# Output projection in token-major blocks with summed pairs, and a sixth summed pair and a residual in PSUM for down: a Hymba layer on one core

## The chip, the cores and the metric

One core of one Trainium2 chip runs the whole program. The metric is the device time of one execution in microseconds; several executions are taken, and the median of them is the kernel's time. The profile is of one further execution, and has a time of its own. The engines are TensorE (PE; PEld is its weight load), VectorE (DVE), ScalarE (ACT), GpSimd (POOL) and SyncE (SP), which here issues nearly all DMAs.

## The reference

One decoder layer, sequence 256, model width 2048, feed-forward width 5632, all in float32:

```python
u = rmsnorm(h)
[lru_x | lru_gate | q | k | v | ret_gate] = u @ W_in
A = rg_lru(causal_conv(lru_x)) * gelu(lru_gate)        # 1024 wide
B = group_norm(retention(q, k, v)) * swish(ret_gate)   # 1024 wide
h = h + concat(A, B) @ W_out                           # the output projection
n = rmsnorm(h)
h = h + (silu(n @ W_gate) * (n @ W_up)) @ W_down       # SwiGLU
out = rmsnorm(h)
```

## The kernel before

Every product of two float32 matrices is done in three passes. Both sides are split into a high part (a cast on ACT, L103, tiles `wh`, `ah`, `bh`) and the rest (a subtraction on DVE, L104, tiles `wl`, `al`, `bl`), and PE adds high x high, high x low and low x high into one PSUM bank (`three`, L653). The weights stream in halves of 512 KB, 128 x 1024 numbers, over SP's queue into five raw buffers (`raw`) and four pairs of split buffers. The program is a list of steps, each with the weight units that it needs; the loads and splits of a step are written out three halves ahead of it (`AHEAD`). A scheduler then sets the order of each engine's instructions by its own estimates, so that the order on an engine is not that of the code.

The steps are, with their time in the profile: the projections of `u` to v, lru_x, k, q, the gates, with scan and retention between them, to 293.4 us; the output projection to 383.8; eleven gate/up blocks to 858.3; two down blocks to 1088.5; the last norm and the stores.

The output projection is feature-major: 16 tiles of 128 features by 256 tokens (`fm_tile` with `w_out`). For each of the 16 slices of y a tile takes one matmul with 512 columns (the high and the low part of y side by side, L144) and one with 256 (L145); the last two tiles take three of 256 (L149 to L151). `out_post` adds the two halves of the bank, adds the result to the residual x in its feature-major tiles, scales a copy of it on ACT (`hf`), splits that into the left sides of the gate/up blocks (`Left`, `hh`), and adds up squares, which two matmuls against ones sum over the features (`norm2`, tile `rms`). Later `resid_tok` turns the residual to token-major with 32 transposes (tile `ht`), since the down blocks add to it in that form.

Gate/up and down blocks are token-major: a block has four PSUM banks `c11`, `c12`, `c21`, `c22` of 128 tokens x 512 columns (first digit: the half of the tokens; second: gate or up, or the left or right 512 columns), and runs over quads, 256 rows of weights by 1024 columns each. A plain quad is 8 products of 128 x 128 by 128 x 512 (`EIGHT`), thus 24 matmuls. A summed pair, as Strassen and Winograd did, has 7 products (21 matmuls) on sums of quarters; DVE makes the sums of the weights (L636, four adds) and of the left side (L536 to L539, tile `s`), which are split as well. From the second gate/up block on, the summed pairs of a block run in two parts: a shared part, four products into four banks that are then combined by four DVE adds (L764 to L768, tiles `p`, `q`), done among the steps of the block before, and a direct part of three products. Block and neighbour take turns with two sets of four banks (`room`). The first gate/up block has one summed pair, in another form, and the others have three or four. A down block has 22 quads, five of them summed (`SUMMED_DOWN`); their results go through `part` tiles and the residual tiles `htok`.

At the end of the second down block the last bank, `c22`, is done in two halves (`c22`, `c22b`). `post` adds them to the residual (L930, L932, L935), `down_post` squares the sum on ACT (L956), works out r = 1/sqrt and a correcting step (L968 to L973), and scales four tiles by r (L978 to L988) and by the last norm's weight `fw`, partly on GpSimd ahead of time (L958). The stores are L989.

Of the kernel before, what the change touches and what calls it, by code (L numbers as in the profile page):

```python
# [31 lines left out]
SUMMED = (2, 3, 4)  # L32
SUMMED_MORE = (1, 2, 3, 4)
SUMMED_FIRST = (2,)
SUMMED_DOWN = (2, 5, 8, 11, 14)
# [3 lines left out]
def tile_hymba_layer(ctx: ExitStack, tc: tile.TileContext, A: dict, out: bass.AP):  # L39
# [4 lines left out]
    apool = ctx.enter_context(tc.tile_pool(name="acts", bufs=58))  # L44
    xpool = ctx.enter_context(tc.tile_pool(name="resid", bufs=10))
# [15 lines left out]
    def act_tile(name, dt=F32):  # L61
        return apool.tile([P, 512], dt, tag="act", name=nm(name))

# [329 lines left out]
    y = [None] * KT  # L393

    def lru_out(n, ps):
# [109 lines left out]
    def ret_y(h):  # L505
        ps = aux("yt")
        for t in range(2):
            o = oo[2 * t + h // 4][:, (h % 4) * P : (h % 4) * P + P]
            pe.transpose(ps[:, t * P : t * P + P], o, ident)
        hl = act_tile("y", F32R)  # L510
        g = gnh[:, h : h + 1]
        act.activation(out=hl[:, :S], in_=ps[:, :S], func=AF.Copy, scale=g)
        v.scalar_tensor_tensor(
            out=hl[:, S:], in0=ps[:, :S], scalar=g, in1=hl[:, :S].bitcast(F32), op0=ALU.mult, op1=ALU.subtract
        )
        y[NLRU + h] = hl
# [3 lines left out]
    hf = [None]  # L520
# [28 lines left out]
    def out_post(f, ps):  # L549
        x = xs(f)  # L550
        if f < KT - 2:
            t = act_tile("op")[:, :S]
            halves(ps, t)
            v.tensor_tensor(out=x, in0=x, in1=t, op=ALU.add)
        else:
            v.tensor_tensor(out=x, in0=ps[:, :S], in1=x, op=ALU.add)
        if f % 2 == 0:
            hf[0] = act_tile("hf")
        act.activation(out=hf[0][:, (f % 2) * S : (f % 2) * S + S], in_=x, func=AF.Copy, scale=col(C_LN2 + f))
        if f % 2:  # L560
            hh[f // 2] = Left(hf[0], f // 2 in SUMMED_MORE)
        sq = sumsq[:, :S] if f == 0 else act_tile("sq")[:, :S]
        act.activation(out=sq, in_=x, func=AF.Square)
        if f:
            v.tensor_tensor(out=sumsq[:, :S], in0=sumsq[:, :S], in1=sq, op=ALU.add)

    def norm2():
        ps = room(1)("rms")
        for t in range(2):
            pe.matmul(ps[:, 2 * t : 2 * t + 2], sumsq[:, t * P : t * P + P], ones[:, 0:2], start=True, stop=True)  # L570
        rsqrt_small(r2_tok, ps[:, 0:4:2], 1.0 / D, 2)

    htok = {}

    def resid_tok(cb, room):
        for t in range(2):
            ps = room("ht")
            for i in range(4):
                pe.transpose(ps[:, i * P : i * P + P], xs(4 * cb + i)[:, t * P : t * P + P], ident)  # L579
            htok[(cb, t)] = xpool.tile([P, 512], F32, tag="xh", name=nm("htok"))  # L580
            act.copy(out=htok[(cb, t)], in_=ps)
# [78 lines left out]
    def block(index, quads, lefts, post, ps, tail=(), after=None, between={}, ordered=False):  # L660
# [7 lines left out]
        for c, c0, cw in tail:  # L668
            todo += [(n, c, a, b, c0, cw, i) for i in range(n, len(quads)) for o, a, b in EIGHT if o == c[:3]]
        firsts, lasts = {}, {}  # L670
        for m, (_, c, *_) in enumerate(todo):
            firsts.setdefault(c, m)
            lasts[c] = m
        at = [0]

        def step(i):
            def run():
                while at[0] < len(todo) and todo[at[0]][0] == i:
                    m, (_, c, a, b, c0, cw, *q) = at[0], todo[at[0]]
# [8 lines left out]
                if after:  # L688
                    after(i)
# [51 lines left out]
    def gu(j, i):  # L741
        return A["w_gu"][j * (KT // 2) + i]

    banks = [{} for _ in range(NB)]
    turns = []
    summed = [SUMMED_MORE if j in (2, 4, 6, 8) else SUMMED for j in range(NB)]
    shared = [[Shared(gu(j, i), True) for i in summed[j]] for j in range(NB)]

    def shared_steps(j):

        ps, n = banks[j], len(summed[j])

        def run(m):
            right = shared[j][m].parts
            for c, a, b in (("c11", "a11", "b11"), ("c22", "s1", "t1"), ("c21", "s3", "t3"), ("c12", "s2", "t2")):
                if m == 0:
                    ps[c] = room(j)(c)
                three(ps[c], hh[summed[j][m]][a], right[b], m == 0, m == n - 1)
            if m < n - 1:
# [10 lines left out]
        return [([shared[j][m]], lambda m=m: run(m)) for m in range(n)]  # L770

    def gate_up(j):

        ps, post = banks[j], ffn_post(j, banks[j])
        ahead = shared_steps(j + 1) if j + 1 < NB else []
        plain = [i for i in range(KT // 2) if i not in summed[j]]

        def direct(m, quad):
# [421 lines left out]
```

## Time and profile before

| | us |
|---|---|
| median of 3 runs (1098.54, 1097.71, 1098.88) | 1098.54 |
| the profiled execution: its time | 1099.06 |
| the profiled execution: its span | 1097.3 |
| PE busy, share of the span | 99% |
| weight load of PE | 83% |
| DVE | 84% |
| ACT | 59% |
| GpSimd | 5% |

The time of the profiled execution holds 1.76 us around its span. PE's busy share is a share of time in which some matmul was under way; matmuls overlap, so it does not tell how many more PE could do. Lines of code in the profile's rows are those of this kernel, and a tile's name stands without its number.

### The profile page before, as it was taken

To read this page: it belongs to the slowest core of one execution; us is meant where nothing else is said; L and a number is where in the kernel's file an instruction comes from. 1 tells how busy PE (TensorE), PEld (TensorE's weight loads), DVE (VectorE), ACT (ScalarE), POOL (GpSimd) and SP (SyncE) were. 2 spreads that over 40 slices of the span, in tenths; PEclk is the share of its full clock that TensorE was granted. 3 is DMA by queue.
4 is the path that set the end of the run, shared out by engine and by line. 5 is a ranking of instruction groups with operands and counts; after the bars stand their busy time and mean duration, and the time that the engine had idled before them with its cause. 6 is when DMAs were issued, how large, how long until landed. Compare 5 with 4: busy or idle time off the path is not lost.

```text
span 1097.3 us, 14827 instructions
## 1 busy us (share of the span) xinstructions
PE 1086.0 (99%) x5289; PEld 914.5 (83%) x5289; DVE 917.4 (84%) x1307; ACT 645.9 (59%) x918; POOL 57.4 (5%) x64
## 2 busy tenths in 40 slices
PE   9999999999999999999999999999999999999996
PEld 7888888888888988888888888888888888878885
DVE  7798799987877799998898998998885989777773
ACT  7766644478665566665565556556654666454552
POOL 0602230000000000000000000000000000020001
PEclk9999999999999999999999999999999999999999
DMA  9755574554565547677677677686686555746662
GB/s 329 239 193 162 171 256 162 171 183 163 177 228 191 185 156 275 209 234 260 218 242 254 218 264 240 228 280 225 229 268 216 174 182 191 241 143 210 222 212 76
DMA packets 67114, 232.56 MB, mean 212 GB/s; under 512 B 7648, under 2 KB 8032, under 8 KB 67040
## 3 DMA queue, kind: packets, MB, share of 16 engines
q1 hardware_dynamic: 66240, 229.52, 62.8%
q0 software_dynamic: 512, 1.57, 0.5%
q8 instruction: 41, 0.67, 0.2%
q10 hardware_dynamic: 288, 0.52, 0.1%
q14 instruction: 33, 0.27, 0.1%
HBM read 229.49 MB, written 2.10 MB: 211 GB/s over the span
## 4 chain that ended last, share of the span: by engine, by line
PE 98%; DVE 1%; DMA 0%; ACT 0%; issue 0%; SPq 0%; DVEq 0%; ACTq 0%
PE c L657 20%; PE c L658 20%; PE c L656 20%; PE fm L144 16%; PE fm L145 8%; PE tm L160 3%; PE tm L161 3%; PE tm L162 3%; PE p L658 1%; PE p L657 1%; PE p L656 1%; PE ft L847 1%; PE fm L151 0%; PE fm L150 0%; PE fm L149 0%; PE ht L579 0%
## 5 line engine op out<-in xcount | busy, mean ns | idle before, releaser
L103 ACT CAST wh<-raw 128x1024 fp32r<-128x1024 f32 (+1 forms) x475 | 451.1, 974 | 356.9 <-DVE raw L636 118.9
L104 DVE TENSOR_TENSOR wl<-raw,wh 128x1024 fp32r<-128x1024 f32 (+1 forms) x475 | 530.4, 1140 | 113.0 <-ACT wh L103 109.0
L657 PE MATMUL c<-wl,ah 128*128 128x512 f32 x770 | 299.3, 390 | 0.8 <-DVE wl L104 0.8
L658 PE MATMUL c<-wh,al 128*128 128x512 f32 x770 | 298.7, 389 | 0.0
L656 PE MATMUL c<-wh,ah 128*128 128x512 f32 x770 | 248.8, 391 | 0.2 <-ACT wh L103 0.2
L144 PE MATMUL fm<-u,wh 128*128 128x512 f32 x512 | 179.9, 396 | 0.0
L657 PEld LDWEIGHTS c<-wl,ah 128*128 128x128 f32 x770 | 144.5, 188 | 31.2 <-DVE wl L104 1.6
L656 PEld LDWEIGHTS c<-wh,ah 128*128 128x128 f32 x770 | 144.1, 188 | 30.9 <-ACT wh L103 1.6
L658 PEld LDWEIGHTS c<-wh,al 128*128 128x128 f32 x770 | 144.5, 188 | 30.0
L145 PE MATMUL fm<-u,wl 128*128 128x256 f32 x512 | 143.4, 280 | 0.0
L144 PEld LDWEIGHTS fm<-u,wh 128*128 128x128 f32 x512 | 96.0, 188 | 22.3
L145 PEld LDWEIGHTS fm<-u,wl 128*128 128x128 f32 x512 | 96.5, 189 | 0.2
L144 PE MATMUL fm<-y,wh 128*128 128x512 f32 x224 | 78.8, 397 | 0.0
L636 DVE TENSOR_TENSOR raw<-raw,raw 128x512 f32<-128x512 f32 x90 | 62.2, 691 | 3.3 <-DMA raw<-in_w_gu 0.9
L636 DVE TENSOR_TENSOR raw<-raw 128x512 f32<-128x512 f32 x90 | 62.1, 690 | 2.3
L145 PE MATMUL fm<-y,wl 128*128 128x256 f32 x224 | 62.5, 281 | 0.0
L657 PE MATMUL c<-wl,sh 128*128 128x512 f32 x147 | 57.2, 389 | 0.0
L658 PE MATMUL c<-wh,sl 128*128 128x512 f32 x147 | 57.2, 389 | 0.0
L958 POOL TENSOR_TENSOR htok<-htok,fw 128x512 f32<-128x512 f32 (+1 forms) x7 | 9.5, 1368 | 899.1 <-ACT junk L956 899.1
L144 PEld LDWEIGHTS fm<-y,wh 128*128 128x128 f32 x224 | 41.9, 188 | 10.1
L656 PE MATMUL c<-wh,sh 128*128 128x512 f32 x147 | 49.9, 392 | 0.0
L161 PE MATMUL tm<-wl,u 128*128 128x512 f32 x128 | 49.4, 398 | 0.0
(253 smaller groups left out, 1201.6 us busy)
## 6 DMA issues: line engine op xcount, KB each, us to landing
raw<-in_w_gu SPq DMA_DIRECT2D x210, 512.0 KB, 5.1
raw<-in_w_down SPq DMA_DIRECT2D x88, 512.0 KB, 4.5
raw<-in_w_out SPq DMA_DIRECT2D x32, 512.0 KB, 4.1
raw<-in_w_lx SPq DMA_DIRECT2D x16, 512.0 KB, 4.3
raw<-in_w_k SPq DMA_DIRECT2D x16, 512.0 KB, 3.9
raw<-in_w_q SPq DMA_DIRECT2D x16, 512.0 KB, 4.3
raw<-in_w_rg SPq DMA_DIRECT2D x16, 512.0 KB, 3.8
raw<-in_w_lg SPq DMA_DIRECT2D x16, 512.0 KB, 3.8
```

The source lines that it names most:

```text
L103: act.copy(out=dst_h, in_=src)
L104: v.tensor_tensor(out=dst_l, in0=src, in1=dst_h.bitcast(F32), op=ALU.subtract)
L144: pe.matmul(ps, wh, hl, start=first, stop=False)
L145: pe.matmul(ps[:, :S], wl, hl[:, :S], start=False, stop=last)
L160: pe.matmul(ps, ah, wh, start=first, stop=False)
L161: pe.matmul(ps, ah, wl, start=False, stop=False)
L162: pe.matmul(ps, al, wh, start=False, stop=last)
L636: v.tensor_tensor(out=dst, in0=a, in1=b, op=ALU.add)
L656: pe.matmul(p, ah, bh, start=first, stop=False, skip_group_check=onto)
L657: pe.matmul(p, ah, bl, start=False, stop=False, skip_group_check=onto)
L658: pe.matmul(p, al, bh, start=False, stop=last, skip_group_check=onto)
L847: pe.transpose(pt[:, o : o + P], g[:, (2 * b + c) * P : (2 * b + c) * P + P], ident)
```

## The change

The output projection becomes two blocks like those of gate/up, of 8 quads each: `w_out` is packed in quads, y is kept as eight pairs of 256 features, split by `Left`, and the second block has two summed pairs, (4, 5). The class `Block` serves all thirteen blocks; `STEPS` gives the order of plain (p), direct (d) and shared (s) steps, an s being a shared part of the next block. The first gate/up block is in the two-part form too, with two summed pairs instead of one. The others keep their number of three or four, with other pairs chosen.

The residual x is loaded a second time, token-major, into `htok` (eight DMAs, new input `x_tok`). `out_post` adds a PSUM bank to it and squares the sum on ACT with an accumulator; the matmuls of `norm2` and the sums of squares on DVE go. `turn` transposes the new residual to feature-major, scales it on ACT and makes the left sides; the transposes of `resid_tok` go.

The down blocks have six summed pairs. In the second one the residual of `c22` is added in PSUM by DVE while products are still to come (`early`), the other half by way of ACT and DVE into `c22b` (`half_over`), whose first product is done ahead of `c11`. `down_post` then reads PSUM directly; the product r x w moves to GpSimd (`rw`) with two-scalar forms on DVE, one multiply by `fw` moves from GpSimd to DVE, and one of the last scalings is shared by DVE and ACT.

The diff, cut to its core:

```diff
-SUMMED = (2, 3, 4)
-SUMMED_MORE = (1, 2, 3, 4)
-SUMMED_FIRST = (2,)
-SUMMED_DOWN = (2, 5, 8, 11, 14)
+SUMMED = ((), (4, 5), (2, 3)) + ((1, 2, 3), (0, 1, 2, 3)) * 4 + ((1, 2, 3), (1, 2, 3))
+SUMMED_OUT, SUMMED_FFN = (4, 5), (0, 1, 2, 3)
+PLAIN = ((4, 5, 6, 7, 0, 1, 2, 3),) * 2 + (tuple(range(8)),) * 11
+STEPS = ("pppspppspp", "pdppsdpspp", "pdpsdpspspp") + ...
+SUMMED_DOWN = (2, 5, 8, 11, 14, 17)
...
+        cb, t = divmod(n, 2)
+        htok[cb, t] = res_tile("htok")
+        nc.sync.dma_start(out=htok[cb, t], in_=A["x_tok"][t * P : t * P + P, cb * 512 : cb * 512 + 512])
...
+        def turn(p):
+            pt, f = room(d)("ht"), act_tile("hf")
+            for c in range(2):
+                for t in range(2):
+                    h = htok[p // 2, t][:, (p % 2) * S + c * P : (p % 2) * S + c * P + P]
+                    pe.transpose(pt[:, c * S + t * P : c * S + t * P + P], h, ident)
+            for c in range(2):
+                cs = slice(c * S, c * S + S)
+                act.activation(out=f[:, cs], in_=pt[:, cs], func=AF.Copy, scale=col(C_LN2 + 2 * p + c))
+            hh[p] = Left(f, p in SUMMED_FFN)
+        def post(c, ps):
+            cb, t = 2 * d + int(c[2]) - 1, int(c[1]) - 1
+            h = htok[cb, t]
+            v.tensor_tensor(out=h, in0=ps, in1=h, op=ALU.add)
+            act.activation(out=act_tile("junk"), in_=h, func=AF.Square, accum_out=sq2[:, t, cb : cb + 1])
+            if t:
+                turns.extend(lambda p=p: turn(p) for p in (2 * cb, 2 * cb + 1))
...
+        def half_over():
+            h = htok[3, 1][:, S:]
+            act.copy(out=h, in_=ps["c22"][:, S:])
+            v.tensor_tensor(out=ps["c22b"][:, S:], in0=ps["c22b"][:, S:], in1=h, op=ALU.add)
+        if d:
+            early["c22"] = lambda: v.tensor_tensor(out=ps["c22"], in0=ps["c22"], in1=htok[3, 1], op=ALU.add)
+            early["c22b"] = half_over
+            tail[:0] = [("c22b", S, S, slice(0, 1))]
+            tail += [("c22", 0, S), ("c22b", S, S, slice(1, 4))]
...
-        v.tensor_scalar(out=r, in0=w, scalar1=r, scalar2=None, op0=ALU.mult)
+        rw = rw3[:, t : t + 1]
+        pool.tensor_tensor(out=rw, in0=r, in1=w, op=ALU.mult)
...
-    for f in range(KT):
-        fm_tile(Unit(A["w_out"][f]), y, order, lambda ps, f=f: out_post(f, ps), one=f >= KT - 2)
+    blocks = [Block(d, lambda i, d=d: A["w_out"][8 * d + i], y, out_post(d), STEPS[d]) for d in range(2)]
```

Three places of the program, before and after. VectorE in the output projection, before: weight splits, and between them one summed left side.

```order
L104 TENSOR_TENSOR wl_705_3603<-raw_703_3601,wh_704_3602 128x1024
L104 TENSOR_TENSOR al_688_3532<-hf_677_3476,ah_687_3531 128x512
L536 TENSOR_TENSOR s_689_3535<-hf_677_3476 128x128
L538 TENSOR_TENSOR s_689_3535<-hf_677_3476 128x128
L537 TENSOR_TENSOR s_689_3535<-hf_677_3476,s_689_3535 128x128
L539 TENSOR_TENSOR s_689_3535<-hf_677_3476,s_689_3535 128x128
L104 TENSOR_TENSOR wl_708_3609<-raw_706_3607,wh_707_3608 128x1024
L104 TENSOR_TENSOR sl_691_3541<-s_689_3535,sh_690_3540 128x512
```

After, where the first block of the output projection ends and the second begins (L583 adds a bank to the residual, L109 is the split):

```order
L583 TENSOR_TENSOR htok_578_2908<-c12_654_3251,htok_578_2908 128x512
L583 TENSOR_TENSOR htok_595_2982<-c22_655_3255,htok_595_2982 128x512
L109 TENSOR_TENSOR wl_721_3581<-raw_719_3578,wh_720_3580 128x1024
L109 TENSOR_TENSOR wl_728_3623<-raw_726_3620,wh_727_3622 128x1024
L109 TENSOR_TENSOR wl_731_3629<-raw_729_3626,wh_730_3628 128x1024
L109 TENSOR_TENSOR al_735_3653<-hf_733_3645,ah_734_3652 128x512
L549 TENSOR_TENSOR s_736_3656<-hf_733_3645 128x128
L551 TENSOR_TENSOR s_736_3656<-hf_733_3645 128x128
L550 TENSOR_TENSOR s_736_3656<-hf_733_3645,s_736_3656 128x128
L552 TENSOR_TENSOR s_736_3656<-hf_733_3645,s_736_3656 128x128
L109 TENSOR_TENSOR wl_762_3743<-raw_760_3740,wh_761_3742 128x1024
L109 TENSOR_TENSOR sl_738_3662<-s_736_3656,sh_737_3661 128x512
```

The left sides of the gate/up blocks now follow one another here, one weight split between the parts of each, where before they came one for every two feature tiles.

SP's queue among the loads for the second projection, before (`gw` are gate weights):

```order
L122 DMA raw_472<-in_w_lx 128x1024
L313 DMA gw_442<-in_gates 128x512
L122 DMA raw_511<-in_w_lx 128x1024
L122 DMA raw_517<-in_w_lx 128x1024
L313 DMA gw_448<-in_gates 128x512
```

After, with the residual's loads (L424):

```order
L127 DMA raw_514<-in_w_lx 128x1024
L424 DMA htok_2850<-in_x_tok 128x512
L424 DMA htok_2908<-in_x_tok 128x512
L424 DMA htok_2982<-in_x_tok 128x512
L424 DMA htok_3053<-in_x_tok 128x512
L424 DMA htok_3114<-in_x_tok 128x512
L424 DMA htok_3172<-in_x_tok 128x512
L424 DMA htok_3233<-in_x_tok 128x512
L127 DMA raw_520<-in_w_lx 128x1024
```

Seven of the eight loads stand between two neighbouring halves of weights.

VectorE at the end, before, from the last additions of the residual on:

```order
L930 TENSOR_TENSOR htok_5832<-c_1912_9246,htok_5832 128x256
L932 TENSOR_TENSOR htok_5832<-c_1912_9246,htok_5832 128x256
L935 TENSOR_TENSOR htok_5832<-c22b_10120,htok_5832 128x256
L963 TENSOR_REDUCE pre<-ssq 128x1
L964 TENSOR_SCALAR pre<-pre 128x1
L969 TENSOR_SCALAR m_121<-ssq,pre 128x1
L970 RECIPROCAL r_122<-r_122 128x1
L971 TENSOR_SCALAR m_121<-m_121,r_122 128x1
L972 TENSOR_SCALAR m_121<-m_121,r_122 128x1
L973 TENSOR_SCALAR r_122<-m_121,r_122 128x1
L988 TENSOR_SCALAR htok_4663<-htok_4663,r_122 128x512
```

After:

```order
L941 TENSOR_REDUCE pre<-ssq 128x1
L942 TENSOR_SCALAR pre<-pre 128x1
L945 TENSOR_SCALAR pre<-ssq,pre 128x1
L946 TENSOR_TENSOR htok_3233<-c_1916_9078,fw_7771 128x256
L951 TENSOR_SCALAR m_123<-ssq,pre 128x1
L952 TENSOR_TENSOR htok_3233<-c22b_9879,fw_7771 128x256
L953 RECIPROCAL r_124<-r_124 128x1
L954 TENSOR_SCALAR m_123<-m_123,r_124 128x1
L955 TENSOR_SCALAR m_123<-m_123,r_124 128x1
L968 TENSOR_SCALAR htok_2850<-htok_2850,r_124,m_123 128x512
```

The three additions are gone from the end; two multiplies by `fw` stand there, behind which the reciprocal and the scalings follow.

More of the change, by code (lines that the diff above doesn't have):

```diff
@@ L567, in norm2 @@
[L567 to L581, printed above, removed]
+    sq2 = cpool.tile([P, 2, 4], F32, name="sq2")
@@ L658, in three, with block @@
         pe.matmul(p, al, bh, start=False, stop=last, skip_group_check=onto)
-    def block(index, quads, lefts, post, ps, tail=(), after=None, between={}, ordered=False):
+    def block(index, quads, lefts, post, ps, tail=(), early={}, ordered=False):
         n = len(quads) - (2 if tail else 0)
@@ L768, in run, with direct @@
             v.tensor_tensor(out=ps["c21"], in0=ps["c21"], in1=p, op=ALU.subtract)
[L770 to L778, printed above, removed]
-            for c, a, b in (("c11", "a12", "b21"), ("c21", "a22", "t4"), ("c12", "s4", "b22")):
-                three(ps[c], hh[summed[j][m]][a], quad.parts[b], False, False, True)
-            if m == 0 and j == NB - 1:
-                load_fw()
-        def rest(n, quad):
-            count = {}
-            for m, (c, a, b) in enumerate(EIGHT if n < len(plain) - 1 else LAST):
-                if n == 0 and m == 4:
+        def direct(self, m, quad):
+            for c, a, b in (("c11", "a12", "b21"), ("c21", "a22", "t4"), ("c12", "s4", "b22")):
+                three(self.ps[c], self.lefts[self.summed[m]][a], quad.parts[b], False, False, True)
@@ L788, in rest, with plain @@
+        def plain(self, i, quad, first, last):
+            ps, onto, seen = self.ps, bool(self.summed), set()
+            for n, (c, a, b) in enumerate(LAST if last else EIGHT):
+                if first and n == 4:
                     while turns:
                         turns.pop(0)()
-                    if j < 5:
-                        resid_tok(j - 1, room(j + 1))
-                count[c] = count.get(c, 0) + 1
-                last = n == len(plain) - 1 and count[c] == 2
-                three(ps[c], hh[plain[n]][a], quad.parts[b], False, last, True)
@@ L795, in rest @@
-                if last:
-                    post(c)
-        orders = {
[4 rows of a table removed]
-        }
-        for kind in orders[len(shared[j]), len(ahead)].split():
-            k = int(kind[1])
-            if kind[0] == "p":
-                quad = Quad(gu(j, plain[k]), False)
-                program.append(([quad], lambda n=k, quad=quad: rest(n, quad)))
-            elif kind[0] == "s":
-                program.append(ahead[k])
-            else:
-                quad = Direct(shared[j][k])
-                program.append(([quad], lambda m=k, quad=quad: direct(m, quad)))
@@ L816, in gate_up_first @@
[L816 to L840 removed]
+                start = c not in ps
@@ new lines, in plain, with put @@
+                if start:
+                    ps[c] = room(self.index)(c)
+                stop = last and c in seen
+                three(ps[c], self.lefts[i][a], quad.parts[b], start, stop, onto)
+                seen.add(c)
+                if stop:
+                    self.post(c, ps[c])
+        def put(self, after):
+            plain = [i for i in PLAIN[self.index] if i not in self.summed]
+            for k, kind in enumerate(self.steps):
+                if kind == "p":
+                    i, n = plain.pop(0), len(plain)
+                    quad = Quad(self.src(i), False)
+                    run = lambda i=i, quad=quad, k=k, n=n: self.plain(i, quad, k == 0, n == 0)
+                elif kind == "d":
+                    m = self.steps[:k].count("d")
+                    quad = Direct(self.shared[m])
+                    run = lambda m=m, quad=quad: self.direct(m, quad)
+                else:
+                    m = self.steps[:k].count("s")
+                    quad = after.shared[m]
+                    run = lambda m=m: after.share(m)
+                program.append(([quad], run))
```

235 lines of the change are left out of this document (103 added, 132 removed), and 4 rows, old and new, of the table orders.

## The prediction

> **What bounds the kernel now.** I read the page first: busy shares, the chain that ended last, the clock.
>
> ```profile
> PE 1086.0 (99%) x5289; PEld 914.5 (83%) x5289; DVE 917.4 (84%) x1307; ACT 645.9 (59%) x918; POOL 57.4 (5%) x64
> DVE  7798799987877799998898998998885989777773
> PEclk9999999999999999999999999999999999999999
> PE 98%; DVE 1%; DMA 0%; ACT 0%; issue 0%; SPq 0%; DVEq 0%; ACTq 0%
> ```
>
> TensorE (PE) is 98% of the chain at full clock. A busy PE could still be a PE that is fed just in time, so the waits come next: what PE waited for, in total, times, longest.
>
> ```profile
> PE warm L96 <- DVE eps_t L89: 1.0, 1, 1.0
> PE c L657 <- DVE wl L104: 0.8, 1, 0.8
> PE tm L160 <- ACT u L281: 0.5, 1, 0.5
> PE c L656 <- ACT wh L103: 0.2, 1, 0.2
> ```
>
> 2.5 us in the whole program. So matmul slots that go away are time that goes away, as long as VectorE (DVE, 84%) still keeps ahead. How close DVE is differs by stage; the windows are the early loads, the output projection, the first gate/up block, the next one, the two down blocks, the tail:
>
> ```profile
> core 0: us, PE busy (x) PEld busy (x) DVE busy (x) ACT busy (x) POOL busy (x), PEclk, DMA share, GB/s
> 293.35:383.85 90.50, 90.50 (x547) 80.22 (x546) 64.22 (x106) 53.16 (x88) 0.00 (x0) 1.00 0.60 195
> 383.85:441.54 57.69, 57.69 (x259) 47.33 (x258) 56.14 (x80) 36.04 (x49) 0.00 (x0) 1.00 0.61 206
> 441.54:488.93 47.39, 47.39 (x220) 39.23 (x219) 43.65 (x55) 29.51 (x40) 0.00 (x0) 1.00 0.70 233
> 858.27:972.67 114.40, 113.41 (x501) 92.83 (x500) 93.42 (x122) 65.17 (x83) 3.69 (x3) 1.00 0.56 188
> 972.67:1085.47 112.80, 112.80 (x497) 93.39 (x498) 82.82 (x94) 55.06 (x66) 3.83 (x3) 1.00 0.56 182
> 1085.47:1097.30 11.83, 3.03 (x25) 2.82 (x23) 6.26 (x18) 3.37 (x9) 3.76 (x3) 0.78 0.49 177
> ```
>
> DVE has 26 us to spare in the output projection, 1.6 in the first gate/up block (97% busy, yet PE did not wait), 3.7 in the next, 20 to 30 in each down block.
>
> **The output projection on PE.** Starts of neighbouring matmuls give the price of a slot: first the old form, then the 512-column slot of the blocks.
>
> ```profile
> 293.41 0.39 PE L144 MATMUL fm<-y,wh 128*128 128x512 f32 x1
> 293.64 0.28 PE L145 MATMUL fm<-y,wl 128*128 128x256 f32 x1
> 293.75 0.39 PE L144 MATMUL fm<-y,wh 128*128 128x512 f32 x1
> 383.82 0.40 PE L656 MATMUL c<-wh,ah 128*128 128x512 f32 x1
> 1075.73 0.39 PE L658 MATMUL c<-wh,al 128*128 128x512 f32 x1
> 1085.47 0.28 PE L656 MATMUL c<-bh,ah 128*128 128x256 f32 x1
> ```
>
> The durations (0.39, 0.28) overlap and are no price; the spacing is. From 1075.73 to 1085.47 stand 43 slots of 512 columns: 9.74/43 = 0.2265 us. The old pair costs 0.34 here (293.41 to 293.75). The whole stage, 224 such pairs and 96 matmuls of 256 columns, takes 383.82 - 293.41 = 90.41 us; with 0.12 for a lone slot of 256 columns (23 of them between 1085.47 and the row of 1088.22 further down) that is 0.352 a pair on the mean. The new stage is 2 blocks of 8 quads of 24 matmuls, less 3 for each of the two summed pairs: 378 slots x 0.2265 = 85.62. Saved: **-4.8**. The columns fed fall only from 224 x 768 + 96 x 256 to 378 x 512, by 1.5%; counted by columns at 0.2265 for 512 the old stage would be 87.0 us, and its own 90.41 stands 3.4 above that. This 3.4 goes with the short slots if it is their fixed part (0.12 against half of 0.2265, 0.113), and stays if it belongs to the place in the program. I take it as gone, since the blocks show 0.2265 at their start and at their end; the other end is a saving of 1.4.
>
> [...]
>
> **Three more summed pairs.** One in the first gate/up block (1 to 2), one in each down block (5 to 6): 3 x 3 slots x 0.2265 = **-2.0**.
>
> **The norm's matmuls and the transposes.** The rms matmuls of the second norm leave PE, and 32 transposes of x (8 in 0.87 us) give place to 32 of the new residual: **-0.4** and 0.
>
> ```profile
> L570 PE MATMUL rms<-ones,sumsq x4: 169/251/251, 400.4 to 400.7; 128*128 128x2 f32 x4
> 441.54 0.87 PE ht L579 x8
> ```
>
> PE alone: -4.8 - 2.0 - 0.4 = -7.2.
>
> **What DVE has to do for it.** The grouped rows of 383.85 to 1088.5 give its prices (mean ns behind the bar's busy sum), and one boundary row of the down stage stands below them:
>
> ```profile
> L104 DVE TENSOR_TENSOR wl<-raw,wh 128x1024 fp32r<-128x1024 f32 x269 | 326.0, 1230 | 63.8 <-ACT wh L103 62.9
> L636 DVE TENSOR_TENSOR raw<-raw,raw 128x512 f32<-128x512 f32 x90 | 62.2, 691 | 3.3 <-DMA raw<-in_w_gu 0.9
> L104 DVE TENSOR_TENSOR wl<-raw,wh 128x512 fp32r<-128x512 f32 x68 | 46.6, 685 | 8.0 <-ACT wh L103 7.9
> L939 DVE TENSOR_TENSOR htok<-c,htok 128x512 f32<-128x512 f32 x7 | 4.6, 686 | 14.4 <-PE c L658 14.4
> L538 DVE TENSOR_TENSOR s<-ff 128x128 f32<-128x128 f32 x5 | 1.4, 285 | 0.0
> ```
> ```profile
> 970.44 2.18 DVE L104 TENSOR_TENSOR wl<-raw,wh 128x1024 fp32r<-128x1024 f32 x1 [1.15 <-ACT wh L103]
> ```
>
> A plain quad: 2 splits x 1.23 = 2.44. A summed pair beside it: four adds (2.76) and two more splits, so about 6.0 in its shared part and 1.2 in its direct part, 4.7 more than plain. A summed left side: 0.69 + 4 x 0.285 + 0.69 = 2.5. The output projection's adds before (per 256-column tile, 0.42 each) and the splits of y leave.
>
> Block 1 of the output projection, the first gate/up block's shared part beside it: PE 186 slots = 42.1 and 16 transposes 1.75, 43.9 us. DVE 6 plain 14.6 + 2 direct 2.4 + 2 shared 12.1 + 4 adds that combine 2.7 + 4 posts 2.75 + 4 summed left sides 10.0 = 44.6. The block behind it: PE 198 slots and 16 transposes, 46.6; DVE 6 plain 14.6 + 2 direct 2.4 + 3 shared 18.1 + 2.7 + posts 2.75 + 4 plain left sides 2.75 and the gates' 1.5, 44.8. Block 0 ahead: PE 216 slots, 48.9; DVE 8 plain 19.5 + 2 shared 12.1 and some 5 for y's last left sides, 37. So DVE gains 12 us of slack ahead (less what the four split buffers can hold), loses 0.7 in the middle block; all three together 126 of 139.4. The nearest row is the first gate/up block of before, 56.14 of 57.69 without a wait of PE. But there the four left sides were spread over the 90 us of the old stage, now they come in one burst, when block 0's columns are turned. In the new order of DVE I walked rows 486 to 532 with these prices against PE's slots: the split that PE needs comes between 0 and 1 us ahead of it at two places. I take a stall of **+0.7** there; the ends are 0 (as in the old block, 97% busy) and 6.4, which is half of the burst of 10.0 + 2.75 left uncovered.
>
> In the down blocks the extra pair adds 4.7 to 93.4 of 114.4 and to 82.8 of 112.8: cover stays, 0. The wait between the blocks (1.15 us, then a split that took 2.18 instead of 1.23 while GpSimd multiplied) stays as it is, since what stands there is not touched; a second split caught so would cost 0.95.
>
> [...] The change moves one GpSimd multiply to VectorE, at the tail only.
>
> **The residual, loaded again.** Eight DMAs of 256 KB are written in the lru stage, but stand in SP's order among the second projection's loads, seven of them in one row. SP sits there with two issues for 7.20 us, while ACT's squares hold the splits:
>
> ```profile
> 30.00:35.00 5.00, 5.00 (x31) 4.35 (x30) 0.00 (x0) 5.00 (x10) 3.78 (x3) 1.00 0.56 210
> 29.45 7.20 SPq L122 DMA_DIRECT2D raw<-in_w_lx  x2
> 38.57 0.33 SPq L122 DMA_DIRECT2D raw<-in_w_lx  x1
> 30.34 3.76 ACT L291 ACTIVATE sq<-x 128x512 f32<-128x512 f32 x7
> ```
>
> Seven issues x 0.33 = 2.3 us on SP's queue, inside 7.20; 1.8 MB at 210 GB/s are 8.7 us of transfers, with the queues 0.56 full. Behind them wait the next weight halves, and behind those PE. I take 0, since a wait of SP is there to be filled; the other end is 2.3, the issues uncovered.
>
> **The tail.** The last matmul, the chain from it, and what two queues issue:
>
> ```profile
> 1088.22 0.28 PE L658 MATMUL c22b<-bh,al 128*128 128x256 f32 x1
> 1088.94 0.44 DVE htok L935
> 1090.97 0.22 DVE r L973
> 1087.11 6.08 SPq L989 DMA_DIRECT2D out<-htok  x6
> 1092.03 0.88 ACTq L989 DMA_DIRECT2D out<-htok  x2
> ```
>
> With the residual in PSUM, ACT squares right behind the last matmul: 0.44 of L935 goes from the chain, and the product r x w (0.22) goes to GpSimd: -0.7. Against it ACT's two copies now wait for GpSimd's small product (not shown before; between DVE's 0.22 and a few tenths more), ACT copies half a tile more (about 0.4) ahead of its two DMA issues (0.88), and DVE loses that half. SP issues until 1093.19 either way. Net **-0.2**, ends -0.8 (the chain alone) and +0.6 (ACT's queue becomes the last).
>
> **Sum.** -7.2 + 0.7 + 0 + 0 - 0.2 = -6.7. The profiled execution took 1099.06 (span 1097.3 and 1.76 around it), so 1092.4; it lies 0.5 above the median of the runs, 1098.54, so against that **1091.8**.
>
> **Rivals.** B, the burst is felt. Four left sides in a row stand ahead of weight splits in DVE's order, PE's next quad waits 2 to 5 us instead of 0.7. For it: only four split buffers, so DVE's slack of block 0 can't be stored for long. Against: the old block's 97% without a wait. 1093.1 to 1096.1, say 1095.
>
> C, the same and more: 6.4 of burst, or the loads at the start (2.3) with 4 of burst, or the small end of the PE saving with B. The gain is gone: 1097 to 1100.
>
> D, slower: DVE has no lead left at the end of block 0. Then the whole 10.0 + 2.75 stands between PE and its splits; -7.2 + 12.75 - 0.2 = +5.4, 1104. It decides from 9.4 us of uncovered DVE work on (7.2 and the 2.2 that can be told from no change). Against: block 0 has 12 us more PE than DVE work.
>
> [...]
>
> E, better: the slot of the new stage or the tail at its good end, under 1089.5 (-0.6 of tail, no stall, -1).
>
> That the work is not done as said is no rival: the new order of PE has 378 slots in place of the old 546.
>
> **Numbers.** Forecast (1089.5 to 1093.1) 0.61, B 0.19, C 0.11, D 0.06, E 0.03. About 0.2%, 2.2 us, is what runs of this kernel can tell from no change: 1096.3 to 1100.7. So faster is 0.61 + 0.19 + 0.03 = 0.83, same 0.11, slower 0.06. The range from 1089.5 to 1097.5 leaves out E, D and most of C, and holds about 0.83.
>
> **What would show it.** Right: the stretch from the last gate projection to the first gate/up matmul is 85 to 87 us by matmul slots, at a spacing of 0.2265; PE's waits for splits in blocks 0 to 2 sum to 0 to 2 us; down blocks shorter by 0.7 each; from the last matmul to the end 8.6 instead of 8.8. Wrong: waits of PE for DVE in block 1 or 2 that sum to 3 us or more (B to D), PE waits near 40 us that were not there (the loads), a spacing in the new stage away from 0.2265, or a split beside GpSimd that PE waits for.

## The result and the profile after

| | before | after |
|---|---|---|
| median, us | 1098.71 (4 runs, 1097.71 to 1100.39) | 1091.53 (4 runs, 1089.76 to 1092.19) |
| profiled execution: time / span | 1099.06 / 1097.3 | 1089.76 / 1088.0 |

The ratio is 0.9931 with a 95% interval of 0.9913 to 0.9948: 7.2 us faster by the medians. The profiled execution after is the fastest of its four, so that the two traces lie 9.3 us apart. Engines, clock and PE's waits after:

```profile
PE 1077.2 (99%) x5110; PEld 901.9 (83%) x5110; DVE 930.9 (86%) x1312; ACT 651.3 (60%) x918; POOL 57.0 (5%) x65
PEclk9999999999999999999999999999999999999999
```
```profile
PE warm L101 <- DVE eps_t L94: 1.1, 1, 1.1
PE c L666 <- DVE c L778: 0.5, 1, 0.5
PE tm L165 <- ACT u L286: 0.3, 1, 0.3
PE c L666 <- ACT wh L108: 0.3, 1, 0.3
PE p L666 <- ACT bh L108: 0.3, 1, 0.3
```

VectorE has 13.5 us more to do, in a shorter span, and PE waits 2.5 us in all, as before. Where the 9.3 us went is read from windows between marks that both programs have: the start of the last matmul of the gate projections, the first transposes of the gated product (tile `ft`) of the first and of the eleventh gate/up block, the end of the last matmul, the end of the span. Before, then after:

```profile
293.29:441.16 147.87, 147.87 (x800) 127.23 (x798) 120.03 (x186) 88.83 (x135) 0.00 (x0) 1.00 0.61 200
441.16:858.11 416.95, 416.95 (x1896) 345.89 (x1895) 361.87 (x437) 248.36 (x323) 0.00 (x0) 1.00 0.71 239
858.11:1088.50 230.39, 229.40 (x1023) 189.20 (x1021) 179.12 (x221) 121.56 (x151) 9.35 (x7) 1.00 0.56 184
1088.50:1097.30 8.80, 0.00 (x1) 0.00 (x0) 3.54 (x14) 2.04 (x6) 1.93 (x3) 0.70 0.60 215
```
```profile
291.94:437.96 146.02, 145.68 (x658) 120.41 (x657) 123.88 (x173) 92.85 (x136) 0.00 (x0) 1.00 0.65 216
437.96:852.01 414.05, 413.51 (x1863) 342.26 (x1862) 360.49 (x436) 243.62 (x313) 0.00 (x0) 1.00 0.72 240
852.01:1079.94 227.93, 227.60 (x1017) 188.24 (x1015) 188.61 (x241) 125.51 (x159) 9.65 (x8) 1.00 0.56 185
1079.94:1088.00 8.06, 0.00 (x1) 0.00 (x0) 2.90 (x10) 1.89 (x5) 1.36 (x2) 0.75 0.72 255
```

Front: 293.29 to 291.94, -1.35. Output projection and first gate/up block: -1.85, though 3.5 us of transposes moved into it from the next stretch, so -5.35 like for like. Gate/up 2 to 11: -2.90, or +0.6 if those transposes are left out on both sides. Down: -2.46. Tail: -0.74.

These windows were taken for every kernel below; "stretch" means that of the output projection and the first gate/up block. Medians of the kernel before beside them were 1098.05 to 1098.9. Differences against the changed kernel are told from its median of 1091.53 and, since medians of five runs leave about 1 us open, from these windows.

| kernel | median | ratio to before (95%) | stretch | gate/up 2-11 | down | tail |
|---|---|---|---|---|---|---|
| before | 1098.71 | | 147.87 | 416.95 | 230.39 | 8.80 |
| after | 1091.53 | 0.9931 (0.9913 to 0.9948) | 146.02 | 414.05 | 227.93 | 8.06 |
| down6 alone | 1096.90 | 0.9985 (0.9976 to 0.9994) | 148.22 | 417.38 | 228.84 | 8.77 |
| no out sums | 1092.20 | 0.9942 (0.9930 to 0.9955) | 146.63 | 417.12 | 228.22 | 7.55 |
| down8 | 1096.38 | 0.9981 (0.9972 to 0.9991) | 145.99 | 414.79 | 233.31 | 8.04 |
| short slots | 1094.08 | 0.9957 (0.9945 to 0.9970) | 149.53 | 413.88 | 228.00 | 8.04 |
| no residual load | 1093.58 | 0.9959 (0.9945 to 0.9973) | 145.94 | 414.39 | 227.80 | 7.90 |
| old tail | 1092.88 | 0.9947 (0.9933 to 0.9960) | 145.99 | 415.63 | 228.50 | 8.68 |
| burst doubled | 1101.52 | 1.0027 (1.0016 to 1.0038) | 156.31 | 415.13 | 228.82 | 8.01 |
| out3, down 6 and 8 | 1104.44 | 1.0057 (1.0045 to 1.0069) | 149.50 | 413.56 | 238.70 | 7.99 |
| small burst | 1093.67 | 0.9947 (0.9934 to 0.9961) | 149.23 | 414.85 | 227.12 | 8.04 |
| sums later | 1091.37 | 0.9926 (0.9913 to 0.9939) | 146.10 | 416.16 | 227.52 | 7.99 |
| out3, sums later | 1090.89 | 0.9923 (0.9907 to 0.9939) | 145.95 | 414.70 | 228.71 | 8.00 |
| out3, sums later, down7 | 1092.56 | 0.9949 (0.9936 to 0.9963) | 145.94 | 414.26 | 228.56 | 7.98 |

Controls for reading it: the front of "down6 alone" is the code of before, word for word, and took 291.89 us against 293.29. So the -1.35 of the front is a difference between two executions, not one of the change. Where the code of the stretch is alike, it took 147.87 and 148.22 (the old form, two kernels) and 145.94 to 146.02 (the new form, four kernels). Gate/up 2 to 11 has the same matmuls in all the kernels that follow the changed one and spreads from 413.6 to 417.1; down, with six pairs at the same places, spreads from 227.1 to 228.8. A single trace tells no difference smaller than these spreads.

### The profile page after: what moved, and what is told of

It is laid out like the page before. It is cut to its first block, busy times and chain, and to the rows that moved or that the text cites. A ratio compares the mean times of both kernels' runs of the same rounds, so it can differ in the third digit from the quotient of the medians.

```text
span 1088.0 us, 14501 instructions
## 1 busy us (share of the span) xinstructions
PE 1077.2 (99%) x5110; PEld 901.9 (83%) x5110; DVE 930.9 (86%) x1312; ACT 651.3 (60%) x918; POOL 57.0 (5%) x65
## 4 chain that ended last, share of the span: by engine, by line
PE 93%; DVE 2%; DMA 2%; ACT 1%; issue 1%; SPq 0%; DVEq 0%; ACTq 0%
PE c L667 21%; PE c L666 21%; PE c L668 21%; PE fm L149 11%; PE fm L150 6%; PE tm L165 3%; PE tm L166 3%; PE tm L167 3%; DVE wl L109 1%; DMA raw<-in_w_gu 1%; PE p L666 1%; PE p L667 1%; PE p L668 1%; PE ft L825 1%; ACT wh L108 1%
## 5 line engine op out<-in xcount | busy, mean ns | idle before, releaser
L108 ACT CAST wh<-raw 128x1024 fp32r<-128x1024 f32 (+1 forms) x484 | 458.0, 969 | 357.4 <-DVE raw L646 132.8
L109 DVE TENSOR_TENSOR wl<-raw,wh 128x1024 fp32r<-128x1024 f32 (+1 forms) x484 | 537.2, 1133 | 95.9 <-ACT wh L108 94.0
L668 PE MATMUL c<-wh,al 128*128 128x512 f32 x868 | 337.4, 389 | 0.0
L667 PE MATMUL c<-wl,ah 128*128 128x512 f32 x868 | 337.4, 390 | 0.0
L666 PE MATMUL c<-wh,ah 128*128 128x512 f32 x868 | 284.0, 391 | 0.9 <-DVE c L778 0.5
L666 PEld LDWEIGHTS c<-wh,ah 128*128 128x128 f32 x868 | 162.8, 188 | 35.5 <-DVE c L778 1.3
L668 PEld LDWEIGHTS c<-wh,al 128*128 128x128 f32 x868 | 163.0, 188 | 33.9
L667 PEld LDWEIGHTS c<-wl,ah 128*128 128x128 f32 x868 | 163.0, 188 | 33.2
L937 POOL TENSOR_TENSOR htok<-htok,fw 128x512 f32<-128x512 f32 x6 | 9.3, 1570 | 891.9 <-DMA raw<-in_w_down 786.7
L167 PE MATMUL tm<-wh,u 128*128 128x512 f32 x128 | 48.8, 390 | 0.0
L165 PE MATMUL tm<-wh,u 128*128 128x512 f32 x128 | 45.9, 396 | 0.4 <-ACT u L286 0.3
L667 PEld LDWEIGHTS c<-wl,sh 128*128 128x128 f32 x164 | 30.8, 188 | 6.4
```

Source lines behind the costliest of these rows:

```text
L108: act.copy(out=dst_h, in_=src)
L109: v.tensor_tensor(out=dst_l, in0=src, in1=dst_h.bitcast(F32), op=ALU.subtract)
L165: pe.matmul(ps, ah, wh, start=first, stop=False)
L167: pe.matmul(ps, al, wh, start=False, stop=last)
L666: pe.matmul(p, ah, bh, start=first, stop=False, skip_group_check=onto)
L667: pe.matmul(p, ah, bl, start=False, stop=False, skip_group_check=onto)
```

## The experiments

**Down alone.** The kernel before with

```diff
-SUMMED_DOWN = (2, 5, 8, 11, 14)
+SUMMED_DOWN = (2, 5, 8, 11, 14, 17)
```

> The kernel before with one number changed: a sixth summed pair (17) in both down blocks, nothing else. Theory 'slots': 6 matmul slots of 0.2265 us go, the four adds and two splits per pair hide beside PE: 1.4 us faster than before, about 1097.2, and PE's wait of 0.8 us at the seam of the two down blocks is still there. Rival 'seam': the extra pair also shifts the splits at the seam, and the wait goes with it: 2.2 to 2.4 us faster. Rival 'VectorE': the added 9.4 us of VectorE work come through: 0 or slower.

Down went from 230.39 to 228.84, -1.55, the median 1.6 to 2 us down; PE's wait at the seam of the down blocks is there as before:

```profile
PE c L657 <- DVE wl L104: 0.8, 1, 0.8
PE c L656 <- ACT wh L103: 0.4, 2, 0.2
```

Six slots at 0.2265 are 1.36. "Slots" holds; "seam" falls, since the wait is still there, and "VectorE", since the kernel is faster (0.9976 to 0.9994).

**No summed pairs in the output projection.** The changed kernel with

```diff
-SUMMED = ((), (4, 5), (2, 3)) + ...
-SUMMED_OUT, SUMMED_FFN = (4, 5), (0, 1, 2, 3)
-STEPS = ("pppspppspp", "pdppsdpspp", ...
+SUMMED = ((), (), (2, 3)) + ...
+SUMMED_OUT, SUMMED_FFN = (), (0, 1, 2, 3)
+STEPS = ("pppppppp", "pppppsppsp", ...
```

> The changed kernel without the two summed pairs of the output projection (8 plain quads in each of its blocks). Theory 'slots': 6 slots more, +1.4 us, less the 0.3 us stall in the second block of the output projection if that was due to VectorE's load: +1.0 to +1.4 against the changed kernel, still about 5.8 faster than before. Rival 'VectorE': the pairs' 9.4 us of VectorE work hurt more than the slots bring: as fast as the changed kernel or faster.

The stretch took 0.61 longer, not 1.36, and PE's wait at its second block (0.34 us, ACT's cast `wh`) was gone. So the two pairs bring 0.6 us net: their slots are worth 1.4, and the load that they put on VectorE takes back about half. (Of the 3 us more in gate/up 2 to 11, some 1.6 are waits of PE for a combining add, 2.1 us against 0.5, in code that was not touched.)

**Eight pairs in each down block.** The changed kernel with

```diff
-SUMMED_DOWN = (2, 5, 8, 11, 14, 17)
+SUMMED_DOWN = (2, 4, 6, 8, 11, 13, 15, 18)
```

> The changed kernel with eight summed pairs in each down block instead of six. Theory 'slots': 12 slots fewer, -2.7 us against the changed kernel (about 1088.8), since VectorE has some 15 us to spare in each down block and the two pairs add 9.4. Rival 'VectorE is nearly the bound there': pairs closer together make PE wait for splits, the gain is half or less (0 to -1.3). Rival 'no buffers': PE or the splits wait for free tiles of the activation pool, slower by several us.

Slower by 4.9 us than the changed kernel: down 233.31, +5.4, with 12 slots fewer. The halves of the first down block, after, and here:

```profile
852.10:906.00 53.90, 53.90 (x244) 44.74 (x243) 49.35 (x72) 32.77 (x42) 0.00 (x0) 1.00 0.55 185
906.00:960.00 54.00, 54.00 (x239) 44.40 (x238) 46.48 (x59) 30.85 (x36) 0.00 (x0) 1.00 0.66 217
```
```profile
853.30:907.00 53.70, 51.51 (x228) 41.43 (x227) 51.19 (x78) 33.02 (x43) 0.00 (x0) 1.00 0.56 180
907.00:960.00 53.00, 51.51 (x225) 41.72 (x224) 51.16 (x70) 32.60 (x39) 0.00 (x0) 1.00 0.60 200
```
```profile
PE p L666 <- ACT wh L108: 3.7, 6, 1.2
PE c L667 <- DVE bl L109: 1.1, 1, 1.1
```

VectorE is 95 and 97% busy there, where it was 92 and 86%, and PE's busy time falls below the window. The casts for which PE waits wait in turn for VectorE's sums of the weights, in the same two halves:

```profile
ACT wh L108 <- DVE raw L646: 27.3, 9, 4.0
```

VectorE itself waits there for casts alone (4.0 us), and ACT's waits for PE to give buffers free are 4.4 us where the changed kernel has 6.9, so "no buffers" is out, though its size fits. The rival "VectorE is nearly the bound there" named the cause and missed the size: it had 0 to -1.3, and the kernel lost 4.9. The 15 us of room that the expectation counted were an average over a block.

**Short slots.** The changed kernel, in the output projection's plain and direct products except the first and last into a bank (the call that sets `short` is left out here):

```diff
+        if short and not (first or last):
+            for c in (slice(0, S), slice(S, 512)):
+                pe.matmul(p[:, c], ah, bh[:, c], start=False, stop=False, skip_group_check=True)
+                pe.matmul(p[:, c], ah, bl[:, c], start=False, stop=False, skip_group_check=True)
+                pe.matmul(p[:, c], al, bh[:, c], start=False, stop=False, skip_group_check=True)
+            return
```

> The changed kernel with 300 of the 378 512-column matmuls of the output projection issued as two of 256 columns each, the same columns in all. Theory 'a short slot has a fixed part' (0.12 us for 256 columns against half of 0.2265): 300 x (0.24 - 0.2265) = +3.8 us against the changed kernel, about 1095.3, and the stage's pair spacing 0.24. Rival 'columns only': the 90.4 us of the old stage belonged to its place, not to its short slots: 0. Rival 'weights reloaded': each half loads its own weights again and cannot hide it: +10 or more.

The stretch took 149.53, +3.5, the median +2.6. The spacing is 0.12:

```profile
300.04 0.28 PE L669 MATMUL c<-wl,ah 128*128 128x256 f32 x1
300.16 0.28 PE L670 MATMUL c<-wh,al 128*128 128x256 f32 x1
300.28 0.28 PE L668 MATMUL c<-wh,ah 128*128 128x256 f32 x1
```

300 slots of 512 columns became 600 of 256: 3.5/300 = 0.012 us for each one more, 0.006 for each short one. "Columns only" is out, and so is a weight load that shows. For the 320 short slots of the old stage that makes some 2 of the 3.4 us by which it stood above its columns. The rest lies in its mixed pairs, a slot of 512 and one of 256, at 0.352 us where 0.2265 + 0.12 make 0.3465. This too goes with the form and not with the place: the same pairs of the projections of u take 0.350 us on the mean (497 pairs, before and after alike).

**No load of the residual.** GpSimd fills seven of the eight tiles with zeros instead, so this kernel leaves most of x out of the residual:

```diff
+        if n:
+            pool.memset(htok[cb, t], 0.0)
+        else:
             nc.sync.dma_start(out=htok[cb, t], in_=A["x_tok"][...])
```

> The changed kernel without seven of the eight loads of the token-major residual: GpSimd fills those tiles with zeros instead, so that x is left out of most of the residual. Theory 'hidden': SP's seven issues lie inside a wait of its own and nothing changes: within 0.5 us of the changed kernel. Rival 'issues uncovered': the loads delay the weight halves behind them: up to 2.3 us faster. If the front of the program (start to the first matmul of the output projection) is not shorter, the rival is out.

The front was 294.07, not shorter; PE waited 1.8 us there for GpSimd's sums of squares, which now stood behind the fills. Taken off, 292.3, as in the other kernels that follow the changed one (291.75 to 292.50), which tells nothing below their spread of 0.75 us. The loads themselves, in the changed kernel:

```profile
30.41 5.14 SPq L424 DMA_DIRECT2D htok<-in_x_tok  x7
35.63 0.53 SPq L127 DMA_DIRECT2D raw<-in_w_lx  x1
```

Seven issues took 5.14 us, 0.73 on the mean (single ones 0.39 to 1.42), over twice the 0.33 that the forecast took; the next weight half is issued at 35.63, in the slot that SP spent waiting before (29.45 to 36.65). Hidden, as forecast, with 1.4 us of cover left (7.20 - 2 x 0.33 - 5.14).

**The old tail.** The changed kernel, with the residual of the last column added after the last matmul:

```diff
...
-            early["c22"] = ...
-            early["c22b"] = half_over
-            tail[:0] = [("c22b", S, S, slice(0, 1))]
-            tail += [("c22", 0, S), ("c22b", S, S, slice(1, 4))]
+            tail += [("c22", 0, S), ("c22b", S, S)]
```

> The changed kernel with the residual of the last column added after the last matmul, in two halves as before, instead of in PSUM; six pairs, and the other edits of the tail stay. Theory 'chain': the add of 0.44 us and the wait around it come back between the last matmul and the end: 8.5 to 8.8 us there instead of 8.06, +0.5 to +0.7 in all, and PE's wait at the seam of the down blocks stays away. Rival 'seam': the freed seam (0.8 to 1.0 us) came with this edit, and the wait of before is back: +1.5 or more. Rival 'queues': SP's and ACT's DMA issues set the end, not the chain: 0.

The tail is 8.68, +0.62, as "chain" has it (8.68 to 8.80 in the three kernels with the old tail, 7.55 to 8.06 in the others). The median is 1.35 up; gate/up, where nothing was edited, has +1.6 in this trace. The wait at the seam of the down blocks does not come back; "seam" is out. What the trace of the changed kernel shows there is an earlier split. The first matmuls of the second down block and the split that they need next, before and then after (the split of before, at 970.44, stands in the prediction):

```profile
970.83 1.07 PE L656 MATMUL c<-wh,ah 128*128 128x512 f32 x4
```
```profile
966.10 1.07 PE L666 MATMUL c<-wh,ah 128*128 128x512 f32 x4
963.35 1.82 DVE L109 TENSOR_TENSOR wl<-raw,wh 128x1024 fp32r<-128x1024 f32 x1 [0.89 <-ACT wh L108]
```

Before, the split started 0.39 us ahead of those matmuls, after, 2.75 us, and it still runs beside GpSimd (1.82 us instead of 1.23). So it is no longer late. The kernel with the old tail has the same 2.75 us. Why it comes earlier, in a kernel that changes neither quads nor multiplies there, is open: six pairs alone did not bring it, the tail's edit did not.

**A burst of useless adds.** The changed kernel; `heavy` is set for the four summed left sides of gate/up, N is 4:

```diff
...
+                if heavy:
+                    for _ in range(N):
+                        v.tensor_tensor(out=g, in0=f, in1=f, op=ALU.add)
```

> The changed kernel with 16 more VectorE adds of 0.69 us, four ahead of the sums of each of the four summed left sides that are made in the second block of the output projection: 11.0 us of VectorE work that nobody needs, there alone. Theory 'no lead' (VectorE is 0 to 1 us ahead there, as the forecast has it): PE waits 8 to 10 us in that block and the next, +8 to +10. Rival 'shared lead': VectorE can draw on the 12 us of room in the block before and on the block behind, the scheduler spreads the adds: 0 to +3.

The stretch took 156.31, +10.3 for 11.0 us of VectorE work. "Shared lead" is out. "No lead" has the total, but it gave 8 to 10 us to waits of PE, and these are 7.3, 0.61 and 6.67, where the changed kernel has 0.34. So some 4 of the 11.0 us did not reach PE. The row of that block in the changed kernel looks roomier still:

```profile
343.90:389.80 45.90, 45.55 (x209) 37.46 (x208) 40.77 (x63) 30.72 (x49) 0.00 (x0) 1.00 0.62 208
```
```profile
DVE wl L109 <- ACT wh L108: 5.0, 8, 1.3
```
```profile
ACT wh L108 <- PE c L668: 5.7, 5, 1.9
```

VectorE is idle 5.1 of 45.9 us, in 5.0 of it waiting for ACT's casts, and ACT waits 5.7 for PE to give split buffers free. Read so, idle time of that kind cannot be worked ahead in: the split has no buffer to go to. No kernel here was given more buffers, so this is argued and not shown. The long wait of 6.67 is for `sh`, the cast of a summed left side, and the useless adds stand right ahead of those sums: it is the left side that comes late there. And the stall is dearer than the wait. The rest of the +10.3 is clock:

```profile
377.51 0.79 PE L669 MATMUL c<-wh,sh 128*128 128x512 f32 x1 [6.67 <-ACT sh L108]
378.10 0.63 PE L670 MATMUL c<-wl,sh 128*128 128x512 f32 x1
378.53 0.63 PE L669 MATMUL c<-wh,sh 128*128 128x512 f32 x1
382.37 0.43 PE L671 MATMUL c<-wh,al 128*128 128x512 f32 x1
```
```profile
377.30:382.30 5.00, 4.79 (x11) 3.80 (x12) 4.04 (x6) 3.11 (x6) 0.00 (x0) 0.50 0.00 0
382.30:390.00 7.70, 7.70 (x35) 6.30 (x34) 6.42 (x12) 4.65 (x7) 0.00 (x0) 0.99 0.53 173
```

Behind the wait a slot takes 0.43 instead of 0.2265 for 5 us, at a granted clock of 0.50: 12 slots where 22 would stand, 2.3 to 2.6 us lost.

**Three pairs in the output projection, eight in the second down block alone.**

```diff
+SUMMED = ((), (4, 5, 6), (2, 3)) + ...
+STEPS = ("ppspppsppsp", "pdpdsdpspp", ...
+SUMMED_DOWN = (3, 6, 10, 13, 16, 18), (1, 3, 6, 8, 10, 13, 16, 18)
```

> The changed kernel with a third summed pair in the output projection and eight instead of six in the second down block alone, where VectorE was busy 82.8 of 112.8 us before the change (the first keeps six). Theory 'slots where VectorE has room': 9 slots fewer, -2.0 us against the changed kernel, about 1089.5. Rival 'pairs too close': in the second down block, too, the splits of neighbouring pairs come late as in the kernel with eight in both: +1 to +3.

At 1104.44 this is slower than the kernel before, and 12.9 us above the changed one: the stretch +3.5, down +10.8. In both, what a summed pair needs came late and the clock fell. The waits and the windows around them:

```profile
371.20 0.50 PE L666 MATMUL c<-wh,sh 128*128 128x512 f32 x1 [2.15 <-ACT sh L108]
978.22 0.80 PE L667 MATMUL p<-bl,ah 128*128 128x512 f32 x1 [2.41 <-DVE bl L109]
1084.81 0.50 PE L667 MATMUL c<-bl,ah 128*128 128x512 f32 x1 [1.44 <-DVE bl L109]
```
```profile
371.20:376.00 4.80, 4.75 (x13) 3.45 (x14) 4.02 (x9) 3.26 (x6) 0.00 (x0) 0.64 0.34 109
978.20:983.50 5.30, 5.28 (x12) 4.13 (x13) 5.30 (x6) 2.31 (x3) 0.00 (x0) 0.50 0.38 119
983.50:990.00 6.50, 6.50 (x30) 5.39 (x29) 4.01 (x5) 2.66 (x3) 0.00 (x0) 1.00 0.65 222
```

Both theories missed: the rival had +1 to +3. The second down block, in which VectorE is idle some 26 us, stalls at its first pairs (quads 1 and 3), where GpSimd's multiplies and the additions of the block before lie.

**A small burst.** As above with N = 1, 2.76 us of useless adds.

> As the kernel with the doubled burst, but one extra add of 0.69 us ahead of each of the four summed left sides instead of four: 2.76 us of useless VectorE work in the second block of the output projection. With 11.0 us PE lost 10.3 us there, so VectorE's lead is at most about 1 us. Theory 'no lead, waits alone': +1.8 to +2.8 against the changed kernel. Theory 'waits and clock': where a single wait passes about 2 us the granted clock falls to 0.50 for 4 to 5 us (as behind the waits of 6.67, 2.41 and 2.15 us in two kernels), which adds 2 us: +4 to +5. Waits of 1.3 us and less showed no such fall.

The stretch took 149.23, +3.2, between the two ranges; the median +2.1. One wait of 1.80 us, and behind it the clock, for a shorter time:

```profile
375.40:379.00 3.60, 3.46 (x9) 2.73 (x10) 2.92 (x7) 1.34 (x3) 0.00 (x0) 0.57 0.78 225
379.00:385.00 6.00, 6.00 (x28) 4.93 (x27) 4.32 (x7) 4.01 (x6) 0.00 (x0) 0.97 0.85 295
```

So the wait is 1.8, the slow slots some 1.7. "Waits and clock" has the mechanism right and its size too high, since the slow clock lasted 3.4 us and not 4 to 5; "waits alone" is too low for the trace, though the median would fit it.

**Two of the sums made later, and a third pair on top.** `turn` no longer makes the sums of pairs 0 and 1; they are made at the first step of the second and first gate/up block:

```diff
-            hh[p] = Left(f, p in SUMMED_FFN)
+            hh[p] = Left(f, p in SUMMED_FFN and p > 1)
...
+                    if self.index in (2, 3):
+                        hh[3 - self.index].add_sums()
```

> The changed kernel with the sums of two of the four left sides (pairs 0 and 1) made later, where they are first needed: pair 1 at the start of the first gate/up block, pair 0 at the start of the second; 3.6 us of VectorE work leave the second block of the output projection. Theory 'burst': the last wait there (0.34 us, 0.5 with the slower slots behind it) goes, -0.3 to -0.7 in the stretch of output projection and first gate/up block, 0 elsewhere. Rival 'moved, not gone': the next blocks, where VectorE is 92 to 97% busy, wait instead: 0 to +3.

The wait of 0.34 us in the second block of the output projection is gone, and the stretch is what it was (146.10 against 146.02): a wait of 0.24 stands in the next block instead. No gain, no loss that can be told; the -0.3 to -0.7 did not come. But with the third pair the burst's part shows:

> The kernel with the later sums, and a third summed pair in the output projection; down as in the changed kernel. With three pairs and no later sums the stretch of output projection and first gate/up block took 149.50 us against 146.02. Theory 'burst': with 3.6 us less in the burst the wait of 2.15 us and the slow clock behind it go, and the 3 slots count: 145.3 to 146.0. Rival 'VectorE full': 9.4 us less 3.6 stay on top, the wait and the slow clock stay: 147.5 to 149.5.

145.95 us, where three pairs without later sums took 149.50: the wait of 2.15 and the slow clock are gone, as "burst" has it, at the upper end of its range. Against the changed kernel it is 0.07, not the 0.7 of three slots; two waits of 0.2, with the slower slots behind them, are left. At 1090.89 (0.9923) against 1091.53 (0.9931) the intervals overlap, so this is not shown to be the faster kernel.

> The kernel with the later sums and three pairs in the output projection, and seven summed pairs in each down block (1, 4, 7, 10, 13, 16, 18). With six pairs the down blocks took 227.1 to 228.7 us over several kernels, with eight 233.3 (VectorE 95% busy in the first down block, PE waiting 3.7 us there). Theory 'room up to seven': 6 slots fewer, 226.0 to 227.0, and the whole about 1.4 us faster than the kernel with six, 1089.5. Rival 'the room ends at six': VectorE, 89% busy in the first down block with six pairs, comes late at pairs that are two quads apart: 228.5 to 231, the whole 0 to +2.5.

Down 228.56 with SUMMED_DOWN = (1, 4, 7, 10, 13, 16, 18): 6 slots fewer than with six pairs (228.71, the kernel above) and no time won, with a wait of 1.44 at the first pair of the second down block; the median is 1.7 up. That is what "the room ends at six" has; the spread of 1.7 us in down leaves open whether a little is won or lost.

## Why the prediction was right

1091.8 was forecast, 1091.53 measured. By steps:

- **Output projection, -4.8, with the gate/up sum (-0.7), the norm (-0.4) and a stall of 0.7: -5.2.** Measured -5.35 like for like. Over the two kernels with the old form and the four with the new one it is -5.3 to -5.8. The price of a slot by spacing held, and the choice between 1.4 and 4.8 was settled by the short slots and by the pairs of the projections of u.
- **The stall, +0.7.** One wait, 0.6 us with the slower slots behind it:

```profile
373.10 0.98 PE L666 MATMUL c<-wh,ah 128*128 128x512 f32 x3 [0.34 <-ACT wh L108]
```

  Without the pairs the stretch lost 0.75 us less to such things (1.36 - 0.61). The size was near in part by luck. The forecast added up VectorE's durations, 44.6 us for that block, more than PE had; those of the trace do add up to 44.6, but neighbours overlap, as on PE, and 40.77 of 45.9 us were busy. Its idle time there was waits for ACT's casts (5.0 us). That little lead was left is shown by the two bursts: 2.76 us of useless work raised PE's wait from 0.34 to 1.80, 11.0 us raised it to 7.3. Rival D (slower, 1104) did not come, since the burst itself was covered; but the 12 us of room that were held against it are no reserve: of the work on top of the burst half and more reached PE as waits, the clock added to them, and 11.0 us of it gave 1101.5.
- **Down, -1.4.** The slots are shown by down alone (-1.55). The change has -2.46, since the wait at the seam (0.78 us, 1.05 with the slower slots around it) went, which the forecast held as staying. That step failed: the split comes 2.75 us ahead of the block instead of 0.39. Why it does is open. (Smaller waits elsewhere in down came and went, and nearly cancel.)
- **Gate/up 2 to 11, 0.** +0.6 in the profiled execution, within a spread of 3.5 between kernels with the same work there: combining adds on VectorE (the wait of 0.5 above) come late in one trace and not in another.
- **The residual's loads, 0.** Right, on a price per issue that was less than half of the measured mean.
- **Tail, -0.2.** Mis-sized: -0.74, of which 0.62 by the old tail's run. GpSimd's small product took 0.19 us. ACT's queue did become the last, at 1083.52 against SP's 1083.43, where before SP's was, but by 0.09 us only: the chain's own -0.7 was the value to take.

```profile
1078.97 4.46 SPq L969 DMA_DIRECT2D out<-htok  x6
1082.65 0.87 ACTq L969 DMA_DIRECT2D out<-htok  x2
```

The steps of the two traces sum to -5.35 + 0.6 - 2.46 - 0.74 = -7.95, and -1.35 of the front is not the change's; the medians have -7.2. That the forecast's -6.7 came out so near is in part luck: the seam and the tail brought 1.6 more than forecast, and gate/up and the scatter of executions took most of it back.

On the whole, VectorE's occupancy did not set the time: with 13.5 us more of its work (84% busy before, 86% after) the span is 9.3 us shorter. In one experiment it did locally: with eight pairs in each down block VectorE was 95 and 97% busy in the two halves of the first, and set the time there (PE waited 3.7 us).

## What to carry to other kernels

Price a matmul by the spacing of its neighbours (0.2265 us here, where one of 512 columns lasts 0.39), and prefer few wide ones: here cutting a slot in two cost 0.012 us, and the old form stood 3.4 us above its columns in a stage. Durations overlapped on VectorE too: they add up to 44.6 us where it was busy 40.77, so their sum overstated its load. Before a helper engine is given more work, look for whether its idle time can be worked ahead in; what is read here as a wait for buffers that the bound engine frees was, by the bursts, poor room: with VectorE busy 40.77 of 45.9 us, 11.0 us more of its work raised PE's waits from 0.34 to 7.3 us. Where the last bit of lead was used up, one more pair turned from the -0.7 of its slots to +3.5 in the stretch.

## What was not expected of the hardware

A stall of PE cost more here than its wait. Behind waits of 1.80, 2.15, 2.41 and 6.67 us slots took 0.43 us instead of 0.2265, at a granted clock of 0.50; behind waits of 1.44 us (down7, before 972.12) and 1.19 us (sums later, before 734.86) they did not. Windows cut finer show where the slow clock starts and ends. In the kernel with the small burst:

```profile
372.48:375.89 3.41, 1.59 (x7) 0.98 (x7) 3.41 (x6) 1.48 (x3) 0.00 (x0) 1.00 0.41 126
375.89:379.30 3.41, 3.41 (x10) 2.63 (x9) 2.73 (x6) 1.64 (x4) 0.00 (x0) 0.50 0.76 222
```

The slow stretches lasted 3.41 us (behind 1.80 and behind 2.15), 6.83 (around 2.41) and 10.24 us (around 6.67), once, twice and three times 3.41. In the 3.41 us ahead of each, PE was idle 1.8 to 2.2 us. A single wait of nearly that length left the clock as it was: the kernel without the residual's loads has one of 1.78 us, before 47.43, and keeps a clock of 1.00. Two windows that meet inside that wait have 1.27 and 0.51 us of it:

```profile
43.50:46.92 3.42, 2.15 (x13) 1.59 (x11) 3.42 (x3) 1.10 (x2) 3.26 (x3) 1.00 0.85 273
46.92:50.33 3.41, 2.90 (x18) 2.60 (x19) 3.41 (x5) 2.16 (x3) 0.45 (x1) 1.00 0.56 180
```

So in these runs the clock fell where PE had been idle for 1.8 to 2.2 of 3.41 us, and not behind single waits of 1.78, 1.44 and 1.19 us; what decides between 1.78 and 1.80 is not shown. A single operand that came some 2 us late cost 3 to 4 us (3.2 in the stretch behind the wait of 1.80, 3.5 behind that of 2.15).
